# Five of sixteen up blocks as seven products of quarters, in a hybrid layer on one core of a Trainium2

## The chip, the core and the metric

The program runs on one NeuronCore of a Trainium2 chip. Its engines work side by side, each through its own list of instructions: TensorE (PE, matrix products; PEld is its weight load), VectorE (DVE), ScalarE (ACT), GpSimd (POOL), and SyncE (SP), which here issues the DMAs. Each waits for the others through semaphores. The metric is the device time of one execution in microseconds (us): the median of several runs.

## The reference

A layer for 512 tokens of width 1024, in float32: an input product into an mLSTM and a sparse attention (compressed, selected and window keys), an output product with a residual, a gated feed-forward part with a convolution over three tokens, a gate with a projection of a second input, and a last norm. The part that the change is about:

```python
def conv_ffn(h, w_up, conv_w, conv_b, w_down):
    u = h @ w_up                                  # 512 x 1024 by 1024 x 4096
    gate, val = jnp.split(u, 2, axis=-1)
    gate = lax.conv_general_dilated(gate, conv_w...) + conv_b
    return (jax.nn.silu(gate) * val) @ w_down

x = x + conv_ffn(rms_norm(x, ln2_g[i]), w_up[i], conv_w[i], conv_b[i], w_down[i])
gate = jax.nn.sigmoid(rms_norm(x, ple_norm_g[i]) @ w_ple_gate[i])
x = x + gate * (p[i] @ w_ple_proj[i])
return rms_norm(x, final_g)
```

## The kernel before

Activations lie with features on the 128 partitions and tokens along the free axis: 8 tiles of features (KB) by 512 tokens (S). To keep float32 accuracy every operand is split into a high and a low part, and a product is three matmuls that add up in one PSUM bank: high by high, high by low, low by high (`triple`, and `gemm` from L420 on, which does the first two for all feature tiles and then the third). PE is driven by a stream of jobs (`st`): a job is one block of weights. Its load is issued on SP (`load`), its high part is a copy on ACT and its low part a subtraction on DVE (`split`, L155 and L156), then PE multiplies. `st.prepare(1)` splits the next job while the present one runs. The raw weights have two buffers (`raw`), the split ones two each (`hi`, `lo`). `st.after(us, fn)` puts other work at a due time in the stream's own count of time. The order of PE's list is that of the program (`PE_ORDER`); a scheduler orders the other engines' lists by dependences and by program order.

The stages on PE are: the start (k-tiles of the first product, as their loads come), the input products, attention with the output product, the up stage (16 blocks f of 128 gate and 128 value features, two jobs each, `up_job`), the down stage, the gate product with its first half (`g0` to `g3`) and its second (L1293 to L1295).

Up stage: a job `wu{f}{part}` multiplies one 1024 x 128 block of weights by the residual input scaled by the norm's gains (x2h, x2l), 24 matmuls of 128x512. The norm's root per token (n2rb) comes later, so it is applied in `up_evac` when the bank is read: `zg` for the gate (L1121), `zv` for the value (L1131). Then follow the convolution (ACT L1124, DVE L1125 and L1126, ACT's Silu L1127), the product with the value (L1132), and the split of the result into U (L1134, L1135), which the down stage multiplies.

Start: `first_split(k)` casts and splits tile k of the input and of the first weights; for k=0 the input's first 256 tokens (ACT L367) and the weights' first 292 columns (ACT L371) come first, and PE's first product (L376) needs both.

End: the second half of the gate product is done by token tile t=0..3, the last tile in two pieces of 256 columns. `ple_evac` is tile t's chain: tanh on ACT (L1202), two DVE operations (L1203, L1205), the squares' sum (ACT L1213, or DVE L1210 for the last piece). `finish(t)` makes the norm's root by Newton steps on DVE (L1218 to L1226, names n4{t}...) and scales the row, half on ACT (L1235), half on DVE (L1236). The last tile takes ACT's reciprocal root (n4y, L1243), one Newton step (n4u, n4w) and scales on ACT (L1248) and DVE (L1249); two DMAs write the row.

Of the kernel before, what the change touches and what calls it, by code (L numbers as in the profile page):

```python
# [72 lines left out]
def hybrid_block_kernel(ctx: ExitStack, tc: tile.TileContext, a, out):  # L73
# [37 lines left out]


# [9 lines left out]
    for k, n in ((1, 1), (2, 2), (4, 2), (6, 2)):  # L122
        nc.sync.dma_start(xbuf[:, k:k + n], a["xg"][:, k:k + n])
        nc.sync.dma_start(s1raw[k], a["w_s1"][:, k:k + n])
# [236 lines left out]
    def first_split(k):  # L361
        g = xbuf[:, k, 0:1]
        raw = s1raw[k // 2 * 2 if k > 1 else k][:, k % 2 if k > 1 else 0]
        xcut = ((0, 256), (256, S)) if k == 0 else ((0, S),)
        wcut = ((0, WT), (WT, W1)) if k == 0 else ((0, W1),)
        for c0, c1 in xcut:
            SE.activation(xh[:, k, c0:c1], xbuf[:, k, 2 + c0:2 + c1], AF.Copy, scale=g)  # L367
            VE.scalar_tensor_tensor(xl[:, k, c0:c1], xbuf[:, k, 2 + c0:2 + c1], g, f32(xh[:, k, c0:c1]),
                                    op0=ALU.mult, op1=ALU.subtract)
        for c0, c1 in wcut:  # L370
            i = SE.activation(hi1[:, k % 6, c0:c1], raw[:, c0:c1], AF.Copy)  # L371
# [1028 lines left out]
```

## Time and profile before

| What | Value |
|---|---|
| Time, median of 3 runs | 629.55 us (629.53 to 629.82) |
| Time of the profiled execution | 629.76 us |
| Its span in the trace | 627.4 us |
| Mean granted clock of PE | 0.998 |
| Up stage, from the first `wu` job to the first `wd` | 16 blocks of 48 matmuls of 512 columns |
| DMA | 63.04 MB, mean 100 GB/s |

The span runs from the first to the last instruction that the profiler recorded; 2.4 us of the measured time lie outside it. Rows of the timeline give the start in us, the duration in us, the engine, the line, the operation with output and inputs, the tile's shape, and in brackets the idle time before it with what released it. A duration includes the engine's pipeline, so rows that follow each other closely overlap: the pace of an engine is read from start to start.

### The profile page before, as it was taken

To read this page: it belongs to the slowest core of one execution; us is meant where nothing else is said; L and a number is where in the kernel's file an instruction comes from. 1 tells how busy PE (TensorE), PEld (TensorE's weight loads), DVE (VectorE), ACT (ScalarE), POOL (GpSimd) and SP (SyncE) were. 2 spreads that over 40 slices of the span, in tenths; PEclk is the share of its full clock that TensorE was granted. 3 is DMA by queue.
4 is the path that set the end of the run, shared out by engine and by line. 5 is a ranking of instruction groups with operands and counts; after the bars stand their busy time and mean duration, and the time that the engine had idled before them with its cause. 6 is when DMAs were issued, how large, how long until landed. Compare 5 with 4: busy or idle time off the path is not lost. (4 is left out here: it accounts for less than half of the span.)

```text
span 627.4 us, 8436 instructions
## 1 busy us (share of the span) xinstructions
PE 616.4 (98%) x3021; PEld 501.5 (80%) x3021; DVE 415.6 (66%) x805; ACT 316.1 (50%) x663; POOL 63.4 (10%) x131
## 2 busy tenths in 40 slices
PE   9999999999999999999999999999999999999994
PEld 7888877777777778878888888888888888888884
DVE  6988757787777778872966565655555435345476
ACT  7455556677767756663744333334334223233254
POOL 0400009332333500000000000000000000000000
PEclk9999999999999999999999999999999999999999
DMA  8821136111221423122333322223333322534603
GB/s 315 294 69 69 38 102 157 40 42 61 68 68 34 135 68 101 34 69 67 101 101 100 102 97 85 91 98 101 101 101 101 101 89 82 164 102 140 196 1 135
DMA packets 23066, 63.04 MB, mean 100 GB/s; under 512 B 2728, under 2 KB 7464, under 8 KB 22956
## 3 DMA queue, kind: packets, MB, share of 16 engines
q1 hardware_dynamic: 21488, 59.93, 29.1%
q0 software_dynamic: 1248, 2.16, 1.5%
q8 instruction: 24, 0.39, 0.3%
q10 hardware_dynamic: 288, 0.41, 0.2%
q14 instruction: 18, 0.15, 0.1%
HBM read 56.72 MB, written 2.10 MB: 94 GB/s over the span
## 5 line engine op out<-in xcount | busy, mean ns | idle before, releaser
L790 POOL TENSOR_SCALAR E<-E,rr,sg 128x512 f32<-128x512 f32 (+3 forms) x54 | 38.8, 720 | 71.0 <-DVE rr L785 54.5
L1134 ACT ACTIVATE u<-zv 128x512 fp32r<-128x512 f32 x16 | 10.1, 634 | 45.3 <-DVE zv L1132 45.3
L819 DVE TENSOR_TENSOR pl<-pt,ph 128x512 fp32r<-128x512 f32 x40 | 27.2, 686 | 7.3 <-ACT ph L818 6.7
L1131 DVE TENSOR_TENSOR zv<-pu,n2rb 128x512 f32<-128x512 f32 x16 | 11.0, 690 | 31.3 <-PE pu L433 31.3
L818 ACT ACTIVATE ph<-pt 128x512 fp32r<-128x512 f32 x40 | 23.7, 600 | 15.1 <-PE pt L815 13.8
L1121 DVE TENSOR_TENSOR zg<-pu,n2rb 128x512 f32<-128x512 f32 x16 | 11.1, 692 | 26.0 <-PE pu L433 24.6
L815 PE MATMUL pt<-cols,E 128*128 128x128 f32 x160 | 26.3, 274 | 0.5 <-DVE E L790 0.4
L1120 POOL MEMSET zg<- 128x2 f32 x16 | 1.5, 99 | 243.5 <-DVE cv L1126 150.6
L1161 DVE TENSOR_TENSOR X<-pd,X 128x512 f32<-128x512 f32 x8 | 5.5, 691 | 29.4 <-PE pd L433 29.4
L815 PEld LDWEIGHTS pt<-cols,E 128*128 128x128 f32 x160 | 20.0, 140 | 6.0 <-DVE E L790 0.7
L1124 ACT ACTIVATE cv<-zg,cols 128x512 f32<-128x512 f32 x16 | 13.1, 817 | 20.1 <-DVE zg L1121 20.1
L1127 ACT ACTIVATE cv<-cv 128x512 f32<-128x512 f32 x16 | 10.1, 631 | 24.6 <-DVE cv L1126 24.6
L783 ACT ACTIVATE E<-s,nm 128x384 f32<-128x384 f32 (+2 forms) x48 | 22.1, 470 | 0.0
L823 PE MATMUL pv<-ph,V 128*128 128x512 f32 x40 | 18.8, 470 | 0.0
L1135 DVE TENSOR_TENSOR u<-zv,u 128x512 fp32r<-128x512 f32 x16 | 11.1, 692 | 10.5 <-ACT u L1134 10.5
L825 PE MATMUL pv<-pl,V 128*128 128x512 f32 x40 | 16.5, 412 | 0.1
L785 DVE RECIPROCAL rr<-rs 128x3 f32<-128x3 f32 x32 | 5.5, 171 | 16.7 <-ACT E L783 16.6
L773 DVE TENSOR_REDUCE nm<-s 128x2 f32<-128x768 f32 (+2 forms) x24 | 16.3, 680 | 0.0
L273 DVE TENSOR_TENSOR acc<-acc,sq 128x512 f32<-128x512 f32 x21 | 14.3, 682 | 0.1
L783 ACT ACTIVATE Ec<-s,nm 128x32 f32<-128x32 f32 x24 | 6.8, 282 | 12.3 <-DVE nm L773 9.1
L1126 DVE SCALAR_TENSOR_TENSOR cv<-zg,cols,cv 128x512 f32<-128x512 f32 x16 | 12.0, 751 | 0.5
L1125 DVE SCALAR_TENSOR_TENSOR cv<-zg,cols,cv 128x512 f32<-128x512 f32 x16 | 11.9, 745 | 0.0
(1111 smaller groups left out, 2021.9 us busy)
## 6 DMA issues: line engine op xcount, KB each, us to landing
X<-in_xg SPq DMA_DIRECT2D x1, 2048.0 KB, 8.5
xo<-xturn SPq DMA_DIRECT2D x32, 64.0 KB, 2.0
wgr<-in_w_pg SPq DMA_DIRECT2D x4, 512.0 KB, 3.9
s1r<-in_w_s SPq DMA_DIRECT2D x3, 676.0 KB, 9.0
xT<-in_xg SPq DMA_DIRECT2D x3, 514.0 KB, 8.1
rawx<-in_w_mv SPq DMA_DIRECT2D x3, 512.0 KB, 7.6
Q<-hlq POOLq DMA_DIRECT2D x12, 128.0 KB, 2.8
out_y<-xo SPq DMA_DIRECT2D x3, 512.0 KB, 2.8
```

Source lines behind the costliest of these rows:

```text
L273: return VE.tensor_add(acc[:, :n], acc[:, :n], sq[:, :n])
L773: VE.tensor_reduce(out=nm[:, 1:3], in_=sw, axis=AX.X, op=ALU.max, negate=True)
L783: SE.activation(e, p, AF.Exp, bias=nm[:, b:b + 1], accum_out=rs[:, b:b + 1])
L790: eng.tensor_scalar(e, e, rr[:, b:b + 1], sg[:, i, 3 * h + b:3 * h + b + 1], op0=ALU.mult, op1=ALU.mult)
L815: TE.transpose(pt[:, r * 128:(r + 1) * 128], Es[r][:, c0:c0 + 128], ident)
L818: SE.activation(ph, pt, AF.Copy)
L819: VE.tensor_sub(pl, pt, f32(ph))
L823: TE.matmul(pv, vs, ph, start=first, stop=False)
L825: TE.matmul(pv, vs, pl, start=False, stop=last)
L1124: SE.activation(cv, zg[:, 2:S + 2], AF.Identity, scale=cw(2), bias=cols[:, C_CB + f:C_CB + f + 1])
L1125: VE.scalar_tensor_tensor(cv, zg[:, 1:S + 1], cw(1), cv, op0=ALU.mult, op1=ALU.add)
L1126: VE.scalar_tensor_tensor(cv, zg[:, 0:S], cw(0), cv, op0=ALU.mult, op1=ALU.add)
```

## The change

Five of the up stage's sixteen blocks (FAST: 6, 7, 9, 10, 11) are computed another way. One block is a product of weights (gate, value by two halves of the 1024 features) with the input (two halves of the features by two halves of the tokens): 2 x 2 quarters by 2 x 2 quarters. Plainly that is eight products of quarters; with sums of quarters (Winograd's form of Strassen's product) it is seven, p1 to p7, whose sums give the four quarters of the output. A product of quarters (`seven`) is 4 x 3 matmuls of 256 columns in half a bank.

- Weight sums: four additions of 128x512 on POOL a block (`landed_b`), written to `ws`, which has one buffer and shares the tag of `xturn`. They are split like weights: a block has four jobs, `wu{f}0` (as loaded), `wu{f}s` and `wu{f}t` (sums), `wu{f}1` (half of what was loaded).
- Input sums: 16 additions of 128x256 on POOL into Tf, split into Th and Tl. They need an input that is normalised already: xnh and xnl, made from X on DVE, ACT, DVE in blocks 0 to 3. All blocks from 4 on use it, so their banks are read without n2rb: plain blocks' gates by ACT, values with one DVE operation less. In a changed block the banks are read by seven additions of 256 columns on DVE and one copy on ACT.
- Buffers: `raw` 2 to 4, `hi` and `lo` 2 to 3; from block 6 on jobs are split two ahead and loaded four ahead. The input's low part is two halves (XL0, XL1; `qkhl`, of attention, shares XL1), xnh and x3h lie in `mixa`, xnl and xo share a buffer, the rows of `vo` are 130 wide instead of 132, the scratch space for DMA descriptors is 1024 instead of 2048.
- Start: for k=0 the weights' first cast goes from ACT to DVE, the low part of the input comes ahead of the low part of those weights, and the load of k=1 is two DMAs.
- End: the scaling of row t-1 (`scaled`) comes behind the next tile's `ple_evac`; the last root is formed without the operation n4u; of the last row's ACT half the final 128 columns are scaled on DVE.

```diff
+FAST = (6, 7, 9, 10, 11)
+UNSCALED = 4
+T_XN = 0.4, 4.2
+T_TS = 1.0, 4.5
+AHEAD = 4
+SPLIT = 384
...
-        hi = wpool.tile(shape, F32R, tag="hi", name=name + "h")
-        lo = wpool.tile(shape, F32R, tag="lo", name=name + "l")
+        hi = wpool.tile(shape, F32R, tag="hi", bufs=3, name=name + "h")
+        lo = wpool.tile(shape, F32R, tag="lo", bufs=3, name=name + "l")
...
+                raw = load(name, src, shape) if src is not None else None
+                if landed:
+                    landed(raw)
+                self.loaded.append((name, raw, shape, run, prep))
...
-                self.prepare(1)
+                self.prepare(self.depth)
+                self.load(self.ahead)
...
+        if k == 0:
+            VE.tensor_copy(hi1[:, 0, 0:WT], raw[:, 0:WT])
...
+            elif f < UNSCALED:
+                yield from gemm(ps, wh, wl, range(KB), x2h, x2l, range(KB))
             else:
-                yield from gemm(ps, wh, wl, range(KB), x2h, x2l, range(KB))
+                yield from gemm(ps, wh, wl, range(KB), xnh, xnl, range(KB))
+                up_evac(f, part, ps, None)
+                return
...
+            for q, b in enumerate((0, 4, 1, 5, 2, 6, 3, 7)):
+                st.after(T_XN[0] + T_XN[1] * q, lambda b=b: scaled_input(b))
...
+            if rb2 is None:
+                SE.activation(zg[:, 2:S + 2], ps, AF.Copy)
+            else:
+                VE.tensor_mul(zg[:, 2:S + 2], ps, rb2)
...
-            VE.tensor_mul(zv, ps, rb2)
+            if rb2 is None:
+                VE.tensor_mul(zv, ps, n2["cv"])
+            else:
+                VE.tensor_mul(zv, ps, rb2)
+                VE.tensor_mul(zv, zv, n2["cv"])
+            hidden(f, zv)
+    H = S // 2
+
+    def scaled_input(b):
+        xn = t2k(f"xn{b}")
+        i = VE.scalar_tensor_tensor(xn, X[:, b], cols[:, C_G2 + b:C_G2 + b + 1], n2["rb"], op0=ALU.mult, op1=ALU.mult)
+        SE.activation(xnh[:, b], xn, AF.Copy)
+        VE.tensor_sub(xnl[:, b], xn, f32(xnh[:, b]))
+        n2["xn", b] = xn
+        if b >= 4:
+            j = b - 4
+            top = n2["xn", j]
+            b11, b12, b21, b22 = top[:, 0:H], top[:, H:], xn[:, 0:H], xn[:, H:]
+            t1, t2, t3, t4 = (Tf[:, j, q] for q in range(4))
+            GE.tensor_sub(t1, b12, b11)
+            GE.tensor_sub(t3, b22, b12)
+            GE.tensor_sub(t2, b22, t1)
+            GE.tensor_sub(t4, b21, t2)
+
+    def split_sums(j):
+        SE.activation(Th[:, j], Tf[:, j], AF.Copy)
+        VE.tensor_sub(Tl[j // 2][:, j % 2], Tf[:, j], f32(Th[:, j]))
...
+    def seven(ps, w, x):
+        (wh, wl), (rh, rl) = w, x
+        for j in range(4):
+            TE.matmul(ps, wh[:, j], rh(j), start=j == 0, stop=False)
+            TE.matmul(ps, wh[:, j], rl(j), start=False, stop=False)
+            yield 0.24
+        for j in range(4):
+            TE.matmul(ps, wl[:, j], rh(j), start=False, stop=j == 3)
+            yield 0.12
+
+    def quarter(k0, t0):
+        return (lambda j: xnh[:, k0 + j, t0:t0 + H]), (lambda j: xnl[:, k0 + j, t0:t0 + H])
...
+    def fast_banks(f):
+        fast_turn[0] += 1
+        if fast_turn[0] % 2:
+            ps = [pG(f"pfa{f}"), pT(f"pfb{f}"), pG(f"pfc{f}"), pT(f"pfd{f}")]
+        else:
+            sa = pSa(f"pfa{f}")
+            ps = [sa[:, 0], sa[:, 1], pSb(f"pfc{f}"), pV(f"pfd{f}")]
+        return [p[:, t0:t0 + H] for p in ps for t0 in (0, H)]
+
+    def up_fast(f):
+        d = {}
+        half = lambda w, q: (w[0][:, 4 * q:4 * q + 4], w[1][:, 4 * q:4 * q + 4])
+
+        def landed_a(raw):
+            d["r0"] = raw
+
+        def landed_b(raw):
+            r0, d["r1"] = d["r0"], raw
+            sums = fpool.tile([128, 2, 8, 128], F32, bufs=1, name=f"ws{f}", tag="xturn")
+            s2, s1, s3, s4 = sums[:, 0, 0:4], sums[:, 0, 4:8], sums[:, 1, 0:4], sums[:, 1, 4:8]
+            GE.tensor_add(s1, raw[:, 0:4], raw[:, 4:8])
+            GE.tensor_sub(s2, s1, r0[:, 0:4])
+            GE.tensor_sub(s3, r0[:, 0:4], raw[:, 0:4])
+            GE.tensor_sub(s4, r0[:, 4:8], s2)
+            d["sums"] = sums
+
+        def prep_b(name, raw, shape):
+            return split(name, d["sums"][:, 0], shape)
+
+        def prep_c(name, raw, shape):
+            return split(name, d["sums"][:, 1], shape)
+
+        def prep_d(name, raw, shape):
+            return split(name, d["r1"][:, 4:8], shape)
+
+        def run_a(wh, wl):
+            d["ps"] = fast_banks(f)
+            d["u"] = t2k(f"fu{f}")
+            d["v"] = t2k(f"fv{f}")
+            p1, p2 = d["ps"][0:2]
+            yield from seven(p1, half((wh, wl), 0), quarter(0, 0))
+            v1 = d["v"][:, H:]
+            yield from seven(p2, half((wh, wl), 1), quarter(4, 0))
+            SE.activation(v1, p1, AF.Copy)
+            d["zg"] = gate_rows(f)
+            VE.tensor_add(d["zg"][:, 2:2 + H], p2, v1)
...
+        def run_b(wh, wl):
+            p1, p2, p6, p5 = d["ps"][0:4]
+            u2, u4 = d["u"][:, 0:H], d["v"][:, 0:H]
+            yield from seven(p6, half((wh, wl), 0), tsum(1))
+            yield from seven(p5, half((wh, wl), 1), tsum(0))
+            VE.tensor_add(u2, p6, d["v"][:, H:])
+            VE.tensor_add(u4, p5, u2)
+
+        def run_c(wh, wl):
+            p5, p7, p3 = d["ps"][3:6]
+            u2, u3, u4 = d["u"][:, 0:H], d["u"][:, H:], d["v"][:, 0:H]
+            d["zv"] = fpool.tile([128, S], F32, name=f"zv{f}", tag="zv")
+            yield from seven(p7, half((wh, wl), 0), tsum(2))
+            yield from seven(p3, half((wh, wl), 1), quarter(4, H))
+            VE.tensor_add(d["zg"][:, 2 + H:], p3, u4)
+            convolve(f, d["zg"])
+            VE.tensor_add(u3, p7, u2)
+            VE.tensor_add(d["zv"][:, H:], p5, u3)
+
+        def run_d(wh, wl):
+            zv, p4 = d["zv"], d["ps"][6]
+            yield from seven(p4, (wh, wl), tsum(3))
+            VE.tensor_add(zv[:, 0:H], p4, d["u"][:, H:])
...
+        st.add(f"wu{f}0", a["w_up"][:, f, 0], full, run_a, landed=landed_a)
+        st.add(f"wu{f}s", a["w_up"][:, f, 1], full, run_b, prep_b, landed_b)
+        st.add(f"wu{f}t", None, full, run_c, prep_c)
+        st.add(f"wu{f}1", None, [128, 4, 128], run_d, prep_d)
...
+        if f in FAST:
+            up_fast(f)
+            continue
...
+    st.until(f"wu{min(FAST) - 2}1")
+    st.depth, st.ahead = 2, AHEAD
+    st.until("wu71")
+    U.append(main.tile([128, 2, 4, S], F32R, tag="B16", bufs=3, name="u2"))
...
-            y = newton_column(v, f"n4{t}")
-            SE.activation(xo[:, t, 0], xo[:, t, 0], AF.Copy, scale=y)
-            VE.scalar_tensor_tensor(xo[:, t, 1], xo[:, t, 1], y, gF[:, 1], op0=ALU.mult, op1=ALU.mult)
-            nc.sync.dma_start(orow, xo[:, t])
+            roots[t] = newton_column(v, f"n4{t}")
...
-        SE.activation(y, v, AF.Abs_reciprocal_sqrt)
-        VE.tensor_scalar(u, v, -0.5, None, op0=ALU.mult)
+
+        SE.activation(y, v, AF.Abs_reciprocal_sqrt, scale=-2.0)
         VE.tensor_mul(xo[:, t, 1, CUT:], xo[:, t, 1, CUT:], gF[:, 1, CUT:])
-        VE.scalar_tensor_tensor(w, y, u, y, op0=ALU.mult, op1=ALU.mult)
+        VE.scalar_tensor_tensor(w, y, v, y, op0=ALU.mult, op1=ALU.mult)
         VE.scalar_tensor_tensor(w, w, 1.5, y, op0=ALU.add, op1=ALU.mult)
-        SE.activation(xo[:, t, 0], xo[:, t, 0], AF.Copy, scale=w)
+        SE.activation(xo[:, t, 0, 0:SPLIT], xo[:, t, 0, 0:SPLIT], AF.Copy, scale=w)
+        VE.tensor_scalar(xo[:, t, 0, SPLIT:], xo[:, t, 0, SPLIT:], w, None, op0=ALU.mult)
...
+        y = roots[t]
+        SE.activation(xo[:, t, 0], xo[:, t, 0], AF.Copy, scale=y)
+        i = VE.scalar_tensor_tensor(xo[:, t, 1], xo[:, t, 1], y, gF[:, 1], op0=ALU.mult, op1=ALU.mult)
+        behind(i, added[t + 1], "the next tile's chain comes first")
...
+            if t and not part:
+                scaled(t - 1)
```

More of the change, by code (lines that the diff above doesn't have):

```diff
@@ L110, in t2k, with __init__, __getitem__ @@
         return tmp.tile([128, 512], dt, tag="t2k", name=name)
+    class Halves:
+        def __init__(self, name):
+            self.half = [main.tile([128, 4, S], F32R, tag=f"XL{h}", name=name + "ab"[h]) for h in range(2)]
+        def __getitem__(self, at):
+            p, k, *rest = at
+            return self.half[k // 4][(p, k % 4, *rest)]
     cols = consts.tile([128, N_COLS], F32, name="cols")
@@ L123, in hybrid_block_kernel @@
         nc.sync.dma_start(xbuf[:, k:k + n], a["xg"][:, k:k + n])
[L124 removed]
+        for c0, c1 in ((0, WT), (WT, W1)) if k == 1 else ((0, W1),):
+            nc.sync.dma_start(s1raw[k][:, :, c0:c1], a["w_s1"][:, k:k + n, c0:c1])
     nc.sync.dma_start(cols, a["cols"])
@@ L363, in first_split @@
         raw = s1raw[k // 2 * 2 if k > 1 else k][:, k % 2 if k > 1 else 0]
+        xlow = None
         xcut = ((0, 256), (256, S)) if k == 0 else ((0, S),)
-        wcut = ((0, WT), (WT, W1)) if k == 0 else ((0, W1),)
+        wcut = ((0, WT), (WT, W1)) if k < 2 else ((0, W1),)
+        if k == 0:
+            VE.tensor_copy(hi1[:, 0, 0:WT], raw[:, 0:WT])
         for c0, c1 in xcut:
             SE.activation(xh[:, k, c0:c1], xbuf[:, k, 2 + c0:2 + c1], AF.Copy, scale=g)
-            VE.scalar_tensor_tensor(xl[:, k, c0:c1], xbuf[:, k, 2 + c0:2 + c1], g, f32(xh[:, k, c0:c1]),
-                                    op0=ALU.mult, op1=ALU.subtract)
+            j = VE.scalar_tensor_tensor(xl[:, k, c0:c1], xbuf[:, k, 2 + c0:2 + c1], g, f32(xh[:, k, c0:c1]),
+                                        op0=ALU.mult, op1=ALU.subtract)
+            xlow = xlow or j
         for c0, c1 in wcut:
-            i = SE.activation(hi1[:, k % 6, c0:c1], raw[:, c0:c1], AF.Copy)
-            VE.tensor_sub(lo1[:, k % 6, c0:c1], raw[:, c0:c1], f32(hi1[:, k % 6, c0:c1]))
+            if k or c0:
+                i = SE.activation(hi1[:, k % 6, c0:c1], raw[:, c0:c1], AF.Copy)
+            j = VE.tensor_sub(lo1[:, k % 6, c0:c1], raw[:, c0:c1], f32(hi1[:, k % 6, c0:c1]))
+            if k == 0:
+                behind(j, xlow, "the product of the input's low part comes first")
         return i
@@ L1076, in hybrid_block_kernel @@
     x2h = main.tile([128, KB, S], F32R, tag="XH", name="x2h")
-    x2l = main.tile([128, KB, S], F32R, tag="XL", name="x2l")
+    x2l = Halves("x2l")
     acc2 = tmp.tile([128, 512], F32, tag="acc", bufs=1, name="acc2")
@@ L1117, in up_evac, with hidden @@
+    def hidden(f, zv):
+        uh, ul = U[f // 4][:, 0, f % 4], U[f // 4][:, 1, f % 4]
+        SE.activation(uh, zv, AF.Copy)
+        VE.tensor_sub(ul, zv, f32(uh))
     def up_evac(f, part, ps, rb2):
         if part == 0:
-            zg = fpool.tile([128, S + 2], F32, name=f"zg{f}", tag="zg")
-            GE.memset(zg[:, 0:2], 0.0)
-            VE.tensor_mul(zg[:, 2:S + 2], ps, rb2)
-            cw = lambda j: cols[:, C_CW + 16 * j + f:C_CW + 16 * j + f + 1]
-            cv = fpool.tile([128, S], F32, name=f"cv{f}", tag="cv")
```

98 lines of the change are left out of this document (61 added, 37 removed).

## The prediction

> **What bounds the kernel now.** I read the page's busy table first, then the busy time by windows, then the list of waits, and for durations the timeline rows of one engine at a time.
>
> ```profile
> span 627.4 us, 8436 instructions
> PE 616.4 (98%) x3021; PEld 501.5 (80%) x3021; DVE 415.6 (66%) x805; ACT 316.1 (50%) x663; POOL 63.4 (10%) x131
> ```
>
> PE is busy for 98% of the span. An average can hide stages, so the next view is the windows (columns: length; busy time and instructions of PE, PEld, DVE, ACT, POOL; clock; DMA share; GB/s).
>
> ```profile
> 100.00:150.00 50.00, 49.35 (x271) 39.30 (x270) 38.48 (x86) 35.18 (x109) 22.28 (x38) 1.00 0.26 69
> 410.00:432.00 22.00, 22.00 (x98) 18.21 (x97) 12.72 (x17) 8.19 (x10) 0.20 (x2) 1.00 0.30 96
> 620.00:627.40 7.40, 0.00 (x0) 0.00 (x0) 3.05 (x12) 2.79 (x6) 0.00 (x0) 0.80 0.36 142
> ```
>
> In the up stage (410 to 432) PE has no idle time at all, and DVE is busy for 12.72 of 22 us. In attention (100 to 150) 0.65 of 50 us is lost. The last 7.4 us hold no matmul. So time can come from fewer or cheaper matmuls in the up stage, from the head before PE is fed, and from the tail. Nothing else is a bound now, but something else can become one.
>
> **The seven products.** A step of the old kind and one of the new width:
>
> ```profile
> 420.91 0.39 PE L429 MATMUL pu<-x2h,wu100h 128*128 128x512 f32 x1
> 426.35 0.39 PE L429 MATMUL pu<-x2h,wu101h 128*128 128x512 f32 x1
> 613.49 0.28 PE L1293 MATMUL pg<-wres,x3h 128*128 128x256 f32 x1
> 616.37 0.28 PE L1293 MATMUL pg1last<-wres,x3h 128*128 128x256 f32 x1
> ```
>
> From the first matmul of one part to the first of the next lie 24 matmuls: 5.44 us, 0.2267 each at 512 columns. In the gate product at the end, 24 matmuls of 256 columns take 2.88 us, 0.120 each, each with its own weight load as here. An old block is 48 x 0.2267 = 10.88 us. A changed one is seven products of 4 x 3 matmuls, 84 x 0.120 = 10.08. That is 0.80 a block (0.81 before rounding), and **-4.07 us** for five: the largest term. What it buys is small, 7% of a block, and everything else must stay hidden.
>
> What has to stay hidden stands on DVE. Its paces, from start to start of rows that follow without a gap:
>
> ```profile
> 345.55 1.22 DVE L156 TENSOR_TENSOR wu31l<-wu31r,wu31h 128x1024 fp32r<-128x1024 f32 x1
> 346.69 0.69 DVE L1132 TENSOR_TENSOR zv<-zv,cv 128x512 f32<-128x512 f32 x1
> 322.86 0.69 DVE L1121 TENSOR_TENSOR zg<-pu,n2rb 128x512 f32<-128x512 f32 x1 [1.44 <-ACT n2rb L327]
> 323.47 0.68 DVE L1131 TENSOR_TENSOR zv<-pu,n2rb 128x512 f32<-128x512 f32 x1
> 325.21 0.75 DVE L1125 SCALAR_TENSOR_TENSOR cv<-zg,cols,cv 128x512 f32<-128x512 f32 x1
> 326.00 0.75 DVE L1126 SCALAR_TENSOR_TENSOR cv<-zg,cols,cv 128x512 f32<-128x512 f32 x1
> 617.67 0.42 DVE L1203 SCALAR_TENSOR_TENSOR zz<-zz,ppPL 128x256 f32<-128x256 f32 x1
> 618.00 0.21 DVE L1222 SCALAR_TENSOR_TENSOR n42t<-n42y,n4v 128x1 f32<-128x1 f32 x1
> ```
>
> So a low part of 1024 columns costs 1.14, an operation of 512 costs 0.61, one of 256 costs 0.33, and the convolution's pair 0.79 + 0.75. An old block needs two splits, two scalings out of the banks, the pair, and two more operations: 2.28 + 1.22 + 1.54 + 1.22 = 6.3 of 10.88 us (the window above gives 12.72 / 22 x 10.88 = 6.3). A changed block needs three splits of 1024 and one of 512 (4.03), seven adds of 256 out of the banks (2.31), the pair (1.54) and two of 512 (1.22): **9.1 of 10.08 us**. On DVE, between the end of block 6's gate and block 7, the old program has
>
> ```order
> L1121 TENSOR_TENSOR zg_3943<-pu_3918,n2rb 128x512
> L156 TENSOR_TENSOR wu70l<-wu70r,wu70h 128x1024
> L1125 SCALAR_TENSOR_TENSOR cv_3946<-zg_3943,cols,cv_3946 128x512
> L1126 SCALAR_TENSOR_TENSOR cv_3946<-zg_3943,cols,cv_3946 128x512
> L1131 TENSOR_TENSOR zv_3982<-pu_3957,n2rb 128x512
> L156 TENSOR_TENSOR wu71l<-wu71r,wu71h 128x1024
> L1132 TENSOR_TENSOR zv_3982<-zv_3982,cv_3946 128x512
> L1135 TENSOR_TENSOR u_3430<-zv_3982,u_3430 128x512
> ```
>
> two operations between two splits. In the changed program the same place of DVE (`pf...` are block 6's and 7's banks, `ws` the weight sums, `wu7s` and `wu7t` their splits) reads
>
> ```order
> L1291 TENSOR_TENSOR zg_4030<-pfc_4001,fv_4004 128x256
> L1293 TENSOR_TENSOR fu_4003<-pfc_4001,fu_4003 128x256
> L172 TENSOR_TENSOR wu7sl<-ws_3961,wu7sh 128x1024
> L1159 SCALAR_TENSOR_TENSOR cv_4095<-zg_4030,cols,cv_4095 128x512
> L1294 TENSOR_TENSOR zv_4069<-pfb_4000,fu_4003 128x256
> L1160 SCALAR_TENSOR_TENSOR cv_4095<-zg_4030,cols,cv_4095 128x512
> L1299 TENSOR_TENSOR zv_4069<-pfd_4002,fu_4003 128x256
> L172 TENSOR_TENSOR wu7tl<-ws_3961,wu7th 128x1024
> L1300 TENSOR_TENSOR zv_4069<-zv_4069,cv_4095 128x512
> L1275 TENSOR_TENSOR zg_4160<-pfa_4130,fv_4134 128x256
> L172 TENSOR_TENSOR wu71l<-wu7sr,wu71h 128x512
> ```
>
> The low part of `wu7t` now stands behind the end of block 6, and the first add of block 7 (`zg_4160<-pfa_4130`) behind that. On PE, where one old part simply followed another,
>
> ```order
> L429 MATMUL pu_3882<-x2h,wu51h 128x512
> L430 MATMUL pu_3882<-x2l,wu51h 128x512
> L433 MATMUL pu_3882<-x2h,wu51l 128x512 x8
> L429 MATMUL pu_3918<-x2h,wu60h 128x512
> L430 MATMUL pu_3918<-x2l,wu60h 128x512
> ```
>
> block 7 now runs its third weight job ahead of its second:
>
> ```order
> L1215 MATMUL pfc_4131<-th,wu7th 128x256
> L1216 MATMUL pfc_4131<-tl_3818,wu7th 128x256
> L1215 MATMUL pfd_4132<-th,wu71h 128x256
> L1219 MATMUL pfc_4131<-th,wu7tl 128x256 x4
> L1215 MATMUL pfc_4131<-xnh,wu7th 128x256
> ```
>
> What moved is the due time of `wu7tl`: it is wanted after 24 + 8 + 1 matmuls of block 7, 3.96 us behind block 6's end. Laying both lists out with the durations above, from the start of block 6: DVE delivers `wu7tl` at 14.07 us, PE asks at 10.08 + 3.96 = 14.04; DVE has read bank `pfa` at 15.0, PE wants to write it again (`wu7s`) at about 15.1. That is a schedule with almost no slack.
>
> **The sums on POOL.** Each changed block adds four sums of 128x512 on POOL. The trace has no addition on POOL; the nearest are these rows, and DVE's beside them:
>
> ```profile
> 209.13 0.77 POOL L790 TENSOR_SCALAR E<-E,rr,sg 128x512 f32<-128x512 f32 x1 [3.05 <-DVE rr L785]
> 210.22 1.78 POOL L790 TENSOR_SCALAR E<-E,rr,sg 128x512 f32<-128x512 f32 x1
> 210.15 1.21 DVE L156 TENSOR_TENSOR mq7l<-mq7r,mq7h 128x1024 fp32r<-128x1024 f32 x1
> 211.28 0.68 DVE L819 TENSOR_TENSOR pl<-pt,ph 128x512 fp32r<-128x512 f32 x1
> 212.72 0.80 DVE L972 TENSOR_TENSOR qkhl<-qk,qkhl 128x512 fp32r<-128x512 f32 x1
> ```
>
> The same POOL operation takes 0.77 alone and 1.78 when DVE starts a split of two SBUF tiles at 210.15: it finishes 0.7 after that split does (211.28), while DVE already does `pl`, which reads a bank. So POOL stands still beside DVE operations with two SBUF operands, and works beside those that read a bank. The other way round, `qkhl` takes 0.80 instead of 0.68 behind a POOL operation. A sum has two inputs: at least 0.77, and I put the upper end at twice that, 1.54. I take the middle, **1.15**, 4.6 us a block. Room without harm is DVE's bank adds (2.31) and its idle time (10.08 - 9.1 = 1.0): 3.3 a block. The rest, 1.3, delays DVE in three places, where sums of blocks 7, 10 and 11 fall into a changed block before them (those of 9 fall into plain block 8, where DVE has 4 us free). Against it stands one job split ahead, about 2.9 us, before block 6 and again after block 8. 3 x 1.3 = 3.9 against 5.8 leaves no wait on average, but the two tight due times above miss now and then: I take **+0.5**. At 1.54 it is 3 x (6.2 - 3.3) - 5.8 = **2.9**, the upper end; the lower end is 0.
>
> [...]
>
> **The normalised input.** Blocks from 4 on read eight tiles made while block 0 to 3 run: on DVE 8 x (0.79 + 0.61) = 11.2 us, from 322.86 on.
>
> ```profile
> 322.00:344.00 22.00, 22.00 (x99) 18.22 (x98) 14.66 (x19) 11.96 (x15) 0.30 (x3) 1.00 0.32 107
> 355.83 0.69 DVE L1131 TENSOR_TENSOR zv<-pu,n2rb 128x512 f32<-128x512 f32 x1 [2.17 <-PE pu L433]
> ```
>
> DVE has 7.3 us free in those 22. Pushed through in order, the last tile is done at about 350.6; block 4 starts when block 3's last part ends (355.83) and wants its eighth tile some 3 us later. About 8 us of slack, of which 16 POOL sums of 256 columns could take up to 7 (at 0.45 each): cost 0. Blocks 4 on drop one scaling each, off PE's path: 0.
>
> **Start.**
>
> ```profile
> 3.49 0.51 ACT L367 ACTIVATE x1h<-xT 128x256 fp32r<-128x256 f32 x1 [0.82 <-DMA xT<-in_xg]
> 3.91 0.43 ACT L371 ACTIVATE hi<-s1r 128x292 fp32r<-128x292 f32 x1
> 4.65 1.05 PE L376 MATMUL ptm<-hi,x1h 128*128 128x292 f32 x2
> ```
>
> The first product waits for both casts in a row on ACT. Handing the second to DVE takes at most 0.42 - 0.08 = 0.34 off, at least 0 where DVE then delays the low parts. SP issues one DMA more ahead of the loads from k=2 on, which have 0.7 us of reserve. I take **-0.2**.
>
> **Tail.**
>
> ```profile
> 614.42 0.68 DVE L1203 SCALAR_TENSOR_TENSOR zz<-zz,ppPL 128x512 f32<-128x512 f32 x1
> 615.02 0.74 DVE L1236 SCALAR_TENSOR_TENSOR xo<-xo,n41y,gF 128x512 f32<-128x512 f32 x1
> 615.68 0.68 DVE L1205 TENSOR_TENSOR xo<-xo,zz 128x512 f32<-128x512 f32 x1
> 619.30 0.72 ACT L1235 ACTIVATE xo<-xo,n42y 128x512 f32<-128x512 f32 x1
> 619.92 0.45 ACT L1202 ACTIVATE zz<-pg1last,sc 128x256 f32<-128x256 f32 x1
> 619.12 0.28 PE L1295 MATMUL pg1last<-wres,x3h 128*128 128x256 f32 x1
> 622.21 0.14 DVE L1244 TENSOR_SCALAR n4u<-n4v 128x1 f32<-128x1 f32 x1
> 622.91 0.72 ACT L1248 ACTIVATE xo<-xo,n4w 128x512 f32<-128x512 f32 x1 [0.66 <-DVE n4w L1247]
> ```
>
> The last matmul ends at 619.40, but ACT scales tile 2 until 619.92 before the last tanh. On DVE, tile 1's scaling stands inside tile 2's chain,
>
> ```order
> L1226 SCALAR_TENSOR_TENSOR n41y<-n41t,n41y 128x1
> L1203 SCALAR_TENSOR_TENSOR zz<-zz,ppPL_2625 128x512
> L1236 SCALAR_TENSOR_TENSOR xo<-xo,n41y,gF 128x512
> L1205 TENSOR_TENSOR xo<-xo,zz 128x512
> L1233 SCALAR_TENSOR_TENSOR n4v_5561<-ss,ve 128x1
> ```
>
> and with the change behind the add that tile 2 needs:
>
> ```order
> L1415 SCALAR_TENSOR_TENSOR n41y<-n41t,n41y 128x1
> L1392 SCALAR_TENSOR_TENSOR zz<-zz,ppPL_2629 128x512
> L1394 TENSOR_TENSOR xo<-xo,zz 128x512
> L1443 SCALAR_TENSOR_TENSOR xo<-xo,n41y,gF 128x512
> L1422 SCALAR_TENSOR_TENSOR n4v_5915<-ss,ve 128x1
> ```
>
> Tile 2's add comes 0.66 earlier, so its root and ACT's 0.72 scaling do, and the tanh can start at about 619.45: -0.48. The dropped `n4u` takes out some 0.15, the shorter ACT scaling (384 of 512 columns) some 0.14, half given back because DVE's part before the other output grows: together **-0.7**, bounds -0.3 (tanh gains half, the rest hidden) to -0.8.
>
> **The middle.** Third split buffers, loads further ahead and other buffer sharing reorder attention. The list of waits has for PE there only such rows, of which no more can be won:
>
> ```profile
> PEld pv L825 <- DVE pl L819: 2.1, 8, 0.6
> ```
>
> I take 0, bounds -1.0 and +1.0 (half of that row's sum, or an equal loss).
>
> **Sum**, against the profiled execution (629.76 us, its span 627.4 and 2.4 around it): -4.07 + 0.5 - 0.2 - 0.7 = -4.5, 625.3. The median of the runs is 629.55, 0.2 lower: **625.1**.
>
> **Rivals.**
> 1. *The reserve doesn't hold.* If POOL enters whenever DVE reads a bank and the split ahead is used up at once, all 3 x 1.3 = 3.9 us show instead of 0.5: 628.5. For it: 9.1 of 10.08. Against: the job split ahead.
> 2. *POOL is the bound: slower.* A sum of p us costs 3 x (4p - 3.3) - 5.8 on PE. At p = 1.85 that is 6.5 and the whole gain is gone to beyond 630.8; at 2.3, three times the one-input row, 11.9, **636.5**. Against: nothing in the trace triples for a second operand; DVE's rows don't.
> 3. *Attention or the normalised input comes out worse* by 1.5: 626.6. Against: PE's small waits and the 8 us of slack.
> 4. *The change doesn't do what it says*: 84 matmuls save nothing from 0.1295 us each on (10.88 / 84), for instance if weight loads limit them. Then 629.2. Against: 0.120 in the gate product, with as many loads.
>
> **Numbers.** Forecast 0.70, rivals 0.15, 0.05, 0.07, 0.03. Lower end: no stall, start -0.34, tail -0.8, middle -1.0: 623.3. Upper end: stalls 2.9, start -0.2, tail -0.3: 627.9. The chances take 0.2% as what a measurement can tell from no change, so faster is below 628.29 and slower above 630.81: faster 0.70 + 0.07 + half of rival 1 = 0.85; same the other half and rival 4, 0.10; slower 0.05.
>
> **What would show it.** PE rows of L1215 to L1219 0.120 us apart and a changed block 10.1 us long; PE's windows there full, with DVE near 90%. Waits of PE for `wu7tl`, `wu10tl`, or for DVE's read of `pfa`, would be the stalls, and POOL rows of 2 us and more rival 1's mechanism. The last tanh within 0.1 us of the last matmul shows the tail. The forecast is wrong if sums on POOL take over 1.6 us undisturbed or if DVE's adds out of a bank cost much more than 0.33.

## The result, and the profile after

The changed kernel takes **637.16 us** (median of 4 runs, 635.02 to 637.6), the kernel before 629.59 (629.53 to 629.82): a ratio of 1.0111, 95% interval 1.0098 to 1.0124. It is slower by 7.6 us where 4.5 less were forecast.

The page of the changed kernel, its span and its busy times:

```profile
span 635.8 us, 8936 instructions
PE 620.1 (98%) x3201; PEld 510.9 (80%) x3201; DVE 452.5 (71%) x848; ACT 336.7 (53%) x697; POOL 113.9 (18%) x167
```

PE is as full as before by share, and yet its busy time has grown by 3.7 us where 4.1 us less work was meant: PE works more slowly somewhere. That is not all of the 8.4 us by which the span grew (635.8 against 627.4); the list of PE's waits (engine, tile and line; who released it; us in total, times, longest) has new rows, of which the kernel before has none:

```profile
PE pc L534 <- DVE cXl L522: 2.1, 1, 2.1
PE pfc L1215 <- ACT wu7th L171: 1.7, 1, 1.7
PE pfd L1215 <- ACT wu71h L171: 1.3, 1, 1.3
```

The first is in attention, the others in block 7. The windows around both places (columns as in the prediction; the number behind POOL's count is PE's granted clock) show what came on top:

```profile
64.00:68.00 4.00, 3.80 (x18) 2.90 (x16) 3.87 (x7) 2.96 (x5) 0.00 (x0) 1.00 0.00 0
68.00:72.00 4.00, 2.08 (x24) 2.08 (x25) 3.67 (x6) 2.89 (x5) 0.00 (x0) 0.84 0.00 0
72.00:76.00 4.00, 4.00 (x15) 3.17 (x15) 2.86 (x4) 2.00 (x3) 0.00 (x0) 0.74 0.18 45
...
392.00:396.00 4.00, 2.65 (x21) 2.23 (x19) 2.39 (x5) 2.38 (x3) 2.88 (x2) 1.00 0.23 84
396.00:400.00 4.00, 2.29 (x12) 2.09 (x13) 4.00 (x8) 1.96 (x5) 0.10 (x1) 0.80 0.36 125
400.00:404.00 4.00, 4.00 (x21) 4.00 (x20) 1.29 (x3) 0.42 (x1) 0.00 (x0) 0.50 0.40 131
404.00:408.00 4.00, 4.00 (x31) 4.00 (x30) 1.87 (x3) 2.19 (x3) 3.79 (x3) 0.85 0.02 6
```

From 400 to 404 PE is busy without a gap, at half its clock (0.50). Behind the first wait the clock lost is (0.16 + 0.26) x 4 = 1.7 us, behind the waits of block 7 (0.20 + 0.50 + 0.15) x 4 = 3.4 us. In the kernel before the clock is 1.00 in each of these stretches.

From the first matmuls of the stages, in both traces, where the 8.4 us of span come from (us, rounded one by one):

| Stretch | Before | After | Difference |
|---|---|---|---|
| start to first `wu00` | 310.3 | 314.1 | +3.9 |
| blocks 0 to 5 | 67.1 | 67.0 | -0.1 |
| block 6 (seven products) | 10.9 | 10.2 | -0.7 |
| block 7 (seven products) | 10.9 | 16.7 | +5.8 |
| block 8 | 10.9 | 11.0 | +0.1 |
| blocks 9 to 11 (seven products) | 32.6 | 30.2 | -2.4 |
| blocks 12 to 15 | 43.5 | 44.1 | +0.6 |
| down stage | 88.0 | 89.2 | +1.2 |
| gate product, to the start of PE's last matmul | 44.9 | 45.3 | +0.3 |
| behind that start | 8.3 | 7.9 | -0.4 |

So the seven products do what they should in blocks 9 to 11 (10.07 us each on average). Against them stand three losses: a wait in attention (2.1 and 1.7 of clock), block 7 (3.05 and 3.4 of clock), and a lower pace of matmuls whose code the change doesn't touch (2.3 us from block 8 on, and 0.3 in blocks 4 and 5, which a block 0 shorter by 0.4 hides). The experiments take them one at a time.

### The profile page after: what moved, and what is told of

It reads as the page before. It is cut to its first block, busy times and chain, and to the rows that moved or that the text cites. A ratio compares the mean times of both kernels' runs of the same rounds, so it can differ in the third digit from the quotient of the medians.

```text
span 635.8 us, 8936 instructions
## 1 busy us (share of the span) xinstructions
PE 620.1 (98%) x3201; PEld 510.9 (80%) x3201; DVE 452.5 (71%) x848; ACT 336.7 (53%) x697; POOL 113.9 (18%) x167
## 4 chain that ended last, share of the span: by engine, by line
PE 83%; DVE 10%; ACT 3%; issue 2%; POOL 1%; DVEq 0%; ACTq 0%; POOLq 0%
PE pu L457 5%; PE pu L456 5%; PE pu L460 5%; PE pd L456 5%; PE pd L457 5%; PE pd L460 5%; PE pt L842 2%; PE ptm L403 2%; PE pmq L460 2%; PE pc L407 2%; PE pmq L456 2%; PE pv L850 2%; PE pmq L457 2%; PE pv L852 1%; PE pmo L460 1%
## 5 line engine op out<-in xcount | busy, mean ns | idle before, releaser
L817 POOL TENSOR_SCALAR E<-E,rr,sg 128x512 f32<-128x512 f32 (+3 forms) x54 | 37.3, 691 | 130.1 <-DVE rr L812 121.9
L1161 ACT ACTIVATE cv<-cv 128x512 f32<-128x512 f32 x16 | 10.1, 633 | 31.1 <-DVE cv L1160 31.1
L1166 ACT ACTIVATE u<-zv 128x512 fp32r<-128x512 f32 x16 | 10.1, 633 | 10.4 <-DVE zv L1181 6.8
L1159 DVE SCALAR_TENSOR_TENSOR cv<-zg,cols,cv 128x512 f32<-128x512 f32 x16 | 12.9, 805 | 1.9 <-ACT cv L1158 1.7
L1167 DVE TENSOR_TENSOR u<-zv,u 128x512 fp32r<-128x512 f32 x16 | 14.2, 887 | 0.0
L1181 DVE TENSOR_TENSOR zv<-pu,cv 128x512 f32<-128x512 f32 x7 | 4.8, 691 | 12.0 <-PE pu L460 10.6
L1160 DVE SCALAR_TENSOR_TENSOR cv<-zg,cols,cv 128x512 f32<-128x512 f32 x16 | 12.9, 805 | 0.2
L1043 PE MATMUL mo<-vo,mw 128*128 128x130 f32 x80 | 11.8, 280 | 0.0
```

Of the source, the lines that this page charges most:

```text
L817: eng.tensor_scalar(e, e, rr[:, b:b + 1], sg[:, i, 3 * h + b:3 * h + b + 1], op0=ALU.mult, op1=ALU.mult)
```

## The experiments

### The wait in attention: a pin that lost its meaning

DVE's rows around the wait, first in the kernel before, then in the changed one:

```profile
63.76 1.20 DVE L156 TENSOR_TENSOR mv1l<-rawx,mv1h 128x1024 fp32r<-128x1024 f32 x1
...
66.44 1.19 DVE L495 TENSOR_TENSOR cXl<-cX,cXh 128x992 fp32r<-128x992 f32 x1
67.57 1.23 DVE L156 TENSOR_TENSOR cw10l<-rawx,cw10h 128x1024 fp32r<-128x1024 f32 x1
68.72 0.41 DVE L681 TENSOR_SCALAR gmr<-gf 4x512 fp32r<-4x512 f32 x1
```

```profile
64.85 1.20 DVE L172 TENSOR_TENSOR cw10l<-rawx,cw10h 128x1024 fp32r<-128x1024 f32 x1
...
67.51 0.41 DVE L708 TENSOR_SCALAR gmr<-gf 4x512 fp32r<-4x512 f32 x1
67.96 0.68 DVE L710 SCALAR_TENSOR_TENSOR gmr<-gf,gmr 4x512 fp32r<-4x512 f32 x1
68.68 1.19 DVE L522 TENSOR_TENSOR cXl<-cX,cXh 128x992 fp32r<-128x992 f32 x1
```

The code holds `gmr` behind the split of cw10 (`behind(i, lows["cw10"], ...)`). In the kernel before that split waits for one of two buffers, and so comes behind cXl: the pin held `gmr` behind cXl as well. With three buffers the split goes ahead, the pin is kept to the letter, and cXl, which PE wants at 67.8, stands behind everything. That the third buffer moved the split is read from code and lists; no run changes the number of buffers alone. The run order_fix pins `gmr` behind cXl itself:

```diff
-            VE.tensor_sub(Xl, Xc, f32(Xh))
+            cx["low", kv] = VE.tensor_sub(Xl, Xc, f32(Xh))
...
-        behind(i, lows["cw10"], "the weights come first")
+        behind(i, cx["low", 1], "the blocks come first")
```

> The changed kernel, with the first operation of gmr held behind the low part cXl of the second block's input, instead of behind the split of cw10 (which a third split buffer has moved ahead of cXl). Theory (a pin of the order lost its meaning: PE waits 2.12 us for cXl, and the clock is then at half for 3.41 us): PE's wait at L534 is gone, the clock is 1.00 there, and the up stage starts 3.8 us earlier than in the changed kernel, at 310.3 us; time 637.2 - 3.8 = 633.4. Rival (DVE is simply full there, and something else comes late in cXl's place): a wait of 1 us and more for gmr or the next split, and under 1.5 us gained, 635.7 or more. Rival (the half clock has nothing to do with the wait): 2.1 us gained, 635.1, and the clock still falls to a half for 3.41 us near 70 us.

Measured: 634.13 us (633.23 to 635.25), 3.0 less than the changed kernel; `wu00` starts at 310.8 instead of 314.1. The wait, expected to go, shrinks to

```profile
PE pc L534 <- DVE cXl L522: 0.9, 1, 0.9
```

and the half clock near 70 us is gone: 1.2 us are wait and 1.7 are clock. The cause holds; the 0.9 left is the split of cw10, which still stands ahead of cXl (the run plain, below, moves it and has 0.4 left).

### The lower pace: 128 bytes

The matmuls of one half of a down job, by tile (shortest/median/longest ns, first and last start), in the kernel before and the changed one:

```profile
L429 PE MATMUL pd<-u,wd20h x8: 389/394/402, 508.2 to 512.4; 128*128 128x512 f32 x8
L429 PE MATMUL pd<-u,wd21h x8: 389/389/389, 513.7 to 517.8; 128*128 128x512 f32 x8
```

```profile
L456 PE MATMUL pd<-u,wd20h x8: 392/394/405, 515.7 to 519.9; 128*128 128x512 f32 x8
L456 PE MATMUL pd<-u,wd21h x8: 387/394/398, 521.3 to 525.5; 128*128 128x512 f32 x8
```

Same code, same shapes, no wait; but where the kernel before has 389 ns for each, the changed one scatters around 394. From start to start it is a steady 226.7 ns in the one case and some 232 in the other, with single ones up to 242. In the kernel before, the first half was already so. What differs is where tiles lie. By the addresses of the two programs, modulo 256 bytes, the split weights start at 160 in the kernel before, the tiles of U at 192, 160, 160 and 160; in the changed kernel the weights at 32, U at 64, 160, 160 and 32, xnh at 32 and xnl at 64. The rows of `vo` made 130 wide instead of 132 make its buffer 128 bytes smaller, and shift what lies behind. Three runs test it.

The changed kernel with two paddings (align):

```diff
     xbuf = main.tile([128, KB, S + 2], F32, tag="B16", bufs=3, name="xT")
+    main.tile([128, 32], F32, name="padm")
...
+    fpool.tile([128, 56], F32, name="padf", bufs=1)
     U = [fpool.tile([128, 2, 4, S], F32R, name="u0", bufs=1)]
```

> The changed kernel, with 128 bytes of padding behind the first buffer of main and 224 bytes ahead of fpool, so that every tile that PE streams in the up and down stages (x2, xnh, xnl, U) has the same address modulo 256 bytes as the split weights. Nothing else differs. Theory (the pace of a 512-column matmul depends on the distance of the two operands' addresses modulo 256: 226.7 ns when equal, some 232 else): plain blocks from 4 on 10.88 us instead of 11.03, a pair of down jobs 10.9 instead of 11.15, so 1.1 + 2.0 us in all, time 634.0 (637.2 - 3.1). Rival (the pace falls because two different tiles alternate, or because of other engines' traffic): the same pace as in the changed kernel, 637.2.

Measured: 633.06 us (632.52 to 634.03), 4.1 less, 1.0 more than expected; the two profiled executions differ by 3.6, and the changed kernel's own runs by up to 2.6. Every one of the 384 intervals from start to start in the down stage is 226 or 227 ns. The stage takes 87.0 us instead of 89.2, and 1.0 less than in the kernel before:

```profile
L457 PE MATMUL pd<-u,wd20h x8: 389/389/389, 514.2 to 518.3; 128*128 128x512 f32 x8
L457 PE MATMUL pd<-u,wd21h x8: 389/389/389, 519.7 to 523.7; 128*128 128x512 f32 x8
```

The kernel before, with the narrower `vo` alone:

```diff
-    VW = 4 * 132
+    VW = 4 * 130
...
-        return vo[:, j * VW + h * 132:j * VW + h * 132 + 130]
+        return vo[:, j * VW + h * 130:j * VW + (h + 1) * 130]
```

> The kernel before, with the rows of vo 130 wide instead of 132: its buffer is 128 bytes smaller, which moves two of four tiles of U by 128 bytes against the weights modulo 256, and nothing else of the program. Theory (addresses): the up stage unchanged at 10.88 us a block; the second half of a down job (u2, u3), 24 matmuls, slower by some 0.15 us for u2's part, so the down stage 88.0 us becomes 88.8 to 89.2; time 630.4 to 630.8. Rival (addresses don't matter): 629.6 with every matmul of the second half 226.7 ns as now.

Measured: 631.6 us (631.43 to 632.04), ratio 1.0027 (1.0016 to 1.0038). The up stage is unchanged, the down stage 89.2 us, 1.2 more, as expected. Another 0.4 came in the gate product and 0.7 ahead of the up stage, which was not, so that the time lies 0.8 above the range expected. The second half now scatters too:

```profile
L429 PE MATMUL pd<-u,wd21h x8: 387/394/397, 514.8 to 519.0; 128*128 128x512 f32 x8
```

And the kernel before with u0 moved by 224 bytes:

```diff
+    fpool.tile([128, 56], F32, name="padf", bufs=1)
     U = [fpool.tile([128, 2, 4, S], F32R, name="u0", bufs=1),
```

> The kernel before with 224 bytes of padding ahead of u0, which brings u0 to the same address modulo 256 as the split weights; nothing else. Theory (addresses set the pace): the 512-column matmuls of u0 at 226.7 ns instead of 233, and those of u1 too, which stand behind them; down stage 87.0 us instead of 88.0, time 1.0 less, 628.8. Rival: 629.8.

Measured: 628.93 us (628.39 to 629.42), ratio 0.9983 (0.9974 to 0.9993); the down stage takes 87.0 us, all its matmuls 389 ns. The rival is out: nothing but addresses differs, and the pace follows them each time, on both kernels and in both directions. But it is no rule for a single tile. In the kernel before, u1 starts like the weights (160) and yet runs at 232 to 234 ns with the high weights behind u0, which doesn't (192), in the same job; u2 and u3, in the next job, run at 226.7. In the changed kernel u3 (32, like the weights) runs at 229 to 234 behind u2. One tile that lies apart slows others of its job.

### Block 7: the sums, and who waits for whom

POOL's sums of block 7 in the changed kernel, and the rows of DVE and ACT that met them:

```profile
387.95 1.68 POOL L1250 TENSOR_TENSOR ws<-wu7sr 128x512 f32<-128x512 f32 x1 [2.73 <-DVE wu6tl L172]
389.60 1.74 POOL L1252 TENSOR_TENSOR ws<-wu70r,wu7sr 128x512 f32<-128x512 f32 x1
391.30 2.29 POOL L1251 TENSOR_TENSOR ws<-ws,wu70r 128x512 f32<-128x512 f32 x1
393.67 1.29 POOL L1253 TENSOR_TENSOR ws<-wu70r,ws 128x512 f32<-128x512 f32 x1
...
388.39 1.79 DVE L172 TENSOR_TENSOR wu61l<-wu6sr,wu61h 128x512 fp32r<-128x512 f32 x1
...
393.62 1.06 ACT L171 ACTIVATE wu7sh<-ws 128x1024 fp32r<-128x1024 f32 x1 [4.75 <-POOL ws L1251]
394.59 0.80 ACT L1158 ACTIVATE cv<-zg,cols 128x512 f32<-128x512 f32 x1
395.29 1.04 ACT L171 ACTIVATE wu7th<-ws 128x1024 fp32r<-128x1024 f32 x1
...
396.38 0.39 PE L1215 MATMUL pfc<-th,wu7th 128*128 128x256 f32 x1 [1.73 <-ACT wu7th L171]
```

The sums begin only when block 6's are split (the one buffer `ws`), and take 7.0 us. Only the last, 1.29 us, had DVE quiet beside it; in block 8, with DVE idle, three follow at 1.25. Beside a busy DVE a sum takes 1.7 to 2.3. One DVE operation here takes 1.1 more than alone (wu61l, 1.79 instead of 0.68); the adds out of a bank that run beside the second sum keep their 0.41. The sums end at 394.96; ACT copies wu7t from 395.29 on, and its split is ready 1.7 us after PE wants it (at 394.65).

First the buffer: sums of block 7 in a free buffer of B16 (ws7_apart).

```diff
-            sums = fpool.tile([128, 2, 8, 128], F32, bufs=1, name=f"ws{f}", tag="xturn")
+            if f == 7:
+                sums = main.tile([128, 2, 8, 128], F32, tag="B16", bufs=3, name="ws7")
+            else:
+                sums = fpool.tile([128, 2, 8, 128], F32, bufs=1, name=f"ws{f}", tag="xturn")
```

> The changed kernel, with the weight sums of block 7 in a buffer of their own (a free one of B16), so that they need not wait until block 6's sums are split. Theory (the one buffer ws starts the sums of 7 only at 387.95 us, though their weights landed near 379): POOL makes them from about 380 on, PE's waits for wu7th and wu71h (3.05 us together) go, no half clock (6.83 us) near block 7, block 7 takes 10.1 us instead of 16.7; time 637.2 - 6.5 = 630.7. Rival (POOL is too slow: its four sums take 7 us beside DVE's splits wherever they stand): the wait moves to block 6 or stays over 1.5 us, and 2 us or less are gained, 635 or more. Rival (the sums then delay DVE's splits of block 6): PE waits in block 6.

Measured: 636.83 us (635.77 to 637.68), no gain that can be told. Block 7 takes 10.1 us as expected, but block 6 now 15.7: the sums come earlier (379.79) and delay DVE there.

```profile
380.91 1.78 DVE L1167 TENSOR_TENSOR u<-zv,u 128x512 fp32r<-128x512 f32 x1
382.61 2.31 DVE L172 TENSOR_TENSOR wu6sl<-ws,wu6sh 128x1024 fp32r<-128x1024 f32 x1
384.85 1.78 DVE L1159 SCALAR_TENSOR_TENSOR cv<-zg,cols,cv 128x512 f32<-128x512 f32 x1
386.66 1.65 DVE L1160 SCALAR_TENSOR_TENSOR cv<-zg,cols,cv 128x512 f32<-128x512 f32 x1
```

Four operations in a row are 1.1, 1.1, 1.0 and 0.9 us longer than their kind alone, one for each sum. ACT's split of wu6t stands behind the Silu that waits for them, and PE waits for it, with 3.4 us at half clock behind the wait:

```profile
PE pfc L1215 <- ACT wu6th L171: 2.8, 1, 2.8
```

So a buffer of its own moves the loss from block 7 to block 6 and doesn't end it; the last rival held. In these rows a sum on POOL and a DVE operation with two SBUF inputs take turns: now the one stands still, now the other. Where the sums fall on DVE's two-input operations, each costs DVE 0.9 to 1.1 us, nearly as much as it lasts (1.25). If that is so, the sums are cheaper on DVE itself, at 0.61 us. That is tested with the other two faults removed: by the paddings, and by holding the split of cw10 behind cXl.

```diff
+        if name == "cw10":
+            behind(lows[name], cx["low", 1], "the blocks come first")
```

The five blocks with these two repairs and the sums on POOL (five_pool), and on DVE (five_dve), where `GE` becomes `VE` in the four lines of `landed_b`:

> The changed kernel with its five blocks 6, 7, 9, 10, 11, the padding of align and cXl held ahead of the split of cw10: what is left is block 7. Theory: 628.3 (the run plain) - 4.0 + 3.05 for PE's two waits at block 7 + 1.7 to 3.4 for one or two windows at half clock = 629.0 to 630.8. Rival (the three faults are not independent): a time below 627 or above 632.

> The same, with the four sums of weights of each such block on DVE instead of POOL. Theory (a sum on POOL takes 1.25 us alone, 1.75 beside DVE, and each DVE operation with two SBUF inputs then waits some 1.1 us for it, so that a sum costs DVE more than the 0.61 us that it would take itself): the sums of block 7 take 2.4 us instead of 7.0, its waits go, 628.3 - 4.0 = 624.3, up to 626 with small waits since DVE has 2.4 us a block more in its list. Rival (POOL works beside DVE for the most part, and 9.1 + 2.4 of 10.05 us is too much for DVE): waits of 1 us and more in blocks 7, 10 and 11, over 629.

Measured: 630.18 us (629.41 to 631.42) with POOL, ratio 1.0003 (0.9994 to 1.0013); **625.62 us** (625.59 to 625.97) with DVE, ratio 0.9931 (0.9916 to 0.9946). The two differ in nothing else in the code. The first keeps block 7's waits of 1.7 and 1.3 us and gets another of 0.9 in block 10. Its time lies in the range expected, but not by the sum given there: in the profiled execution no half clock follows the waits at block 7 (columns as above; the clock is 1.00):

```profile
392.00:396.00 4.00, 1.54 (x10) 1.24 (x10) 4.00 (x7) 2.50 (x5) 0.10 (x1) 1.00 0.40 131
396.00:400.00 4.00, 4.00 (x34) 4.00 (x34) 2.05 (x4) 0.84 (x2) 0.00 (x0) 1.00 0.36 111
```

The second has one wait left in these blocks. Its row in the list of waits, two of its sums, and the two rows of ACT ahead of PE's wait:

```profile
PE pfd L1218 <- ACT wu71h L172: 1.3, 1, 1.3
```

```profile
383.04 0.69 DVE L1253 TENSOR_TENSOR ws<-wu7sr 128x512 f32<-128x512 f32 x1
383.64 0.69 DVE L1255 TENSOR_TENSOR ws<-wu70r,wu7sr 128x512 f32<-128x512 f32 x1
...
391.88 0.63 ACT L1164 ACTIVATE cv<-cv 128x512 f32<-128x512 f32 x1 [1.34 <-DVE cv L1163]
392.41 0.61 ACT L172 ACTIVATE wu71h<-wu7sr 128x512 fp32r<-128x512 f32 x1
```

So of the 3.05 us at block 7, 1.7 come from the sums on POOL. The other 1.3 stay without POOL: the copy of wu71h stands in ACT's list behind the Silu of block 6, which waits for the convolution on DVE.

### Which blocks, and what the rest is worth

The remaining runs all have the two repairs. plain has no seven products and no sums; last3, alt4 and run4 differ by `FAST` alone ((9, 10, 11), (6, 8, 10, 11), (6, 8, 9, 10, 11)), with sums on POOL; four_dve has (6, 9, 10, 11) and sums on DVE.

```diff
-FAST = (6, 7, 9, 10, 11)
+FAST = ()
...
-        if b >= 4:
+        if b >= 4 and FAST:
...
-    st.until(f"wu{min(FAST) - 2}1")
-    st.depth, st.ahead = 2, AHEAD
```

> The changed kernel without any seven products (all 16 blocks plain, no sums on POOL, splits one ahead), with the padding of the run align and with the split of cw10 held behind cXl, so that cXl stands ahead of it as in the kernel before. What is left of the change: start, end, normalised input, buffers. Theory: PE has no wait of 0.5 us and more outside the first, up stage at 10.88 us a block, down stage 87.0 us (1.0 less than before, since u0 is aligned too), end 0.4 shorter than before, start up to 0.4: 629.7 - 1.8 = 627.9. Rival (the wait for cXl comes back, or the normalised input makes blocks 0 to 4 late): 629.5 or more.

```diff
-FAST = (6, 7, 9, 10, 11)
+FAST = (9, 10, 11)
```

> The same as plain, with blocks 9, 10 and 11 as seven products. In the changed kernel these three took 10.05 us each without a wait of PE. Theory (a seven-product block is worth 0.8 us as long as no DVE work of the block before is displaced): 627.9 - 2.4 = 625.5, no waits. Rival (what made room for them in the changed kernel was the stall at block 7, which let DVE and POOL run ahead): waits of PE in block 9 or 10 of 1.5 us and more with a half clock behind them, 627 or more.

> The same, with blocks 6, 8, 10 and 11 as seven products: block 6 after the splits of the input's sums, each of the first three behind a plain block, with its own sums made in that block. Theory (the sums alternate with DVE's operations, about 1.1 us each, and fit when the block they fall into is plain): 627.9 - 3.2 = 624.7, no wait over 0.5 us. Rival (they don't fit even there): waits at block 6 or 8, 627 or more.

> The same, with five blocks again: 6, 8, 9, 10 and 11, so block 7 of the changed kernel replaced by block 8. Theory as for alt4: 627.9 - 4.0 = 623.9 if four seven-product blocks in a row hold, since 9 to 11 held; a wait near block 10 or 11 if DVE falls behind by some 1 us a block. Rival (DVE is too full for four in a row): waits of 2 us and more and a half clock from block 9 on, 627 or more.

> The same with blocks 6, 9, 10 and 11 and the sums on DVE. Theory: no waits, 628.3 - 3.2 = 625.1, against 625.5 with three blocks and sums on POOL. Rival (DVE too full): waits in blocks 10 and 11, 627 or more.

| Run | Median us (range) | PE's waits in the up stage |
|---|---|---|
| plain | 628.34 (627.52 to 628.73) | none |
| last3 | 625.54 (625.49 to 625.83) | none |
| alt4 | 627.7 (627.08 to 628.06) | 0.8 and 0.8, both in block 8 |
| run4 | 630.94 (629.84 to 631.91) | 1.9 and 0.8 in block 8, 1.3 and 0.3 in block 10 |
| four_dve | **625.29** (624.99 to 625.49) | none |

Three blocks on POOL are worth 2.8 us (628.34 to 625.54), near the 2.4 expected. My rule for alt4 fell: block 7 is plain there, and the sums of block 8 still make block 8 late, since they fall on block 6's end and on the convolution of block 6 in DVE's list. With 8 to 11 in a row besides 6 (run4), five such blocks cost 2.6 us more than none at all (630.94 to 628.34). With the sums on DVE, four blocks run without a wait; the fifth, block 7, adds nothing (625.62 with five, 625.29 with four). four_dve is faster than both kernels: ratio to the kernel before 0.9924 (0.9909 to 0.9939). Of its 4.6 us, the seven products are worth 3.05 (plain to four_dve); 1.5 are in plain already, and before_align shows 0.95 of that by one padding alone.

## Why the prediction was wrong

- **What bounds the kernel** was right: PE without a gap in the up stage, DVE the engine that would fill.
- **Seven products**: right. A block takes 10.07 us on average where nothing waits (9, 10, 11 in the changed kernel), forecast 10.08. (By the rows shown, 0.80 a block, the term is -4.0; the -4.07 is not in them.)
- **The sums on POOL** is the step that failed in the up stage, in its path and in its size. The price of a sum was near (1.25 us alone, 1.15 taken), and POOL did work beside DVE's bank adds (three of them, at 0.41 or 0.42 us, within the last 1.2 us of block 7's second sum). But the term counted only what the sums delay on DVE, 1.3 us a block, and asked whether DVE delivers the low part wu7tl in time. PE waited for high parts, wu7th and wu71h, which come from ACT. For wu7th the path is POOL's own: the sums of block 7 can't start before the one buffer `ws` is free (387.95), take 7.0 us instead of 4.6 (5.0 if each took the 1.25 of a sum alone) because POOL stands still behind DVE's operations with two SBUF inputs, and are copied on ACT only then. With 4.6 they would have ended at 392.6, 2.1 us before PE asks (an estimate from these rows). The reserve of one job split ahead was none, since the splits that should run ahead wait for the sums. For wu71h it is the order on ACT, whoever makes the sums. Of the waits that the prediction named as signs, the one for DVE's read of `pfa` came only in alt4 (0.8) and run4 (1.9). +0.5 was 3.05 us, just above the upper end of 2.9. The reading that DVE goes first is half of it: in ws7_apart POOL holds up four DVE operations in a row by 0.9 to 1.1 us each. What decides which of the two stands still was not shown.
- **The clock** was not in the sum at all. The profile was read for 1.00 everywhere before, and no term asked what a wait does to it. It added 3.4 us at block 7 and 1.7 in attention.
- **The middle**, at 0 with bounds of 1.0, failed by 3.8 (2.1 of wait and 1.7 of clock): the list of waits before was taken as a bound for what a reordering may cost. It only bounds what can be won. The order of DVE around `gmr` and cXl was there to be read, and the pin in the code named a neighbour, not the instruction that PE needs. The upper end of 627.9 had left out this term's own +1.0 as well.
- **Addresses** were not thought of: 1.2 us in the down stage, 0.3 to 0.4 in the gate, 1.1 in plain blocks from 4 on. The narrower `vo` stood in the diff and was costed at nothing without a word.
- **The normalised input** was right: nothing waits for it in blocks 4 and 5.
- **Start**: 0, not -0.2. The first product begins at 4.64 us, before at 4.65: in this execution ACT's first cast waits for the input's DMA until 3.80 instead of 3.49.
- **Tail**: the tanh of the last piece starts 0.10 us behind PE's last matmul instead of 0.52, as forecast, and the last DMA is issued 0.66 earlier relative to it; but the span behind the last matmul is only 0.4 shorter, and the forecast was 0.7. From that issue to the end of the span it is 4.0 us instead of 3.7; why is open.

```profile
627.89 0.28 PE L1490 MATMUL pg1last<-wres,x3h 128*128 128x256 f32 x1
...
628.27 0.45 ACT L1391 ACTIVATE zz<-pg1last,sc 128x256 f32<-128x256 f32 x1
...
631.78 0.33 SPq L1436 DMA_DIRECT2D out_y<-xo  x1
```

In mechanism rival 1 (the reserve doesn't hold, 3.9 us) came nearest. In number it was rival 2, whose 636.5 for sums of 2.3 us is close to 637.16; that is luck, since a sum takes 1.25 alone and 1.75 on average in block 7, and half of the miss lies in attention and in the pace of matmuls.

## What to carry to other kernels

A saving of 7% of a block on the engine that never waits, 4 us for five blocks, is nearly lost by one wait of 2 us elsewhere when the clock falls behind it (2.1 and 1.7 us here): count each new wait with what may follow it. A pin in an order says "behind this neighbour" and holds only while something else (a buffer count) keeps the neighbour in its place: after a change of buffers, read the order again at each pin. And when a tile changes its size, see where the tiles behind it come to lie.
